# Seven block products of 256 columns in the last feed-forward stage of a decoder trunk

## The chip, the core and the metric

The program runs on one core of a Trainium2 chip. The metric is the device time of one execution in microseconds (us). A core has five engines that work from queues of their own: TensorE (PE, with PEld for its weight loads), VectorE (DVE), ScalarE (ACT), GpSimd (POOL) and SyncE (SP), which here only issues DMAs. PSUM is the memory that TensorE writes its products to; SBUF holds everything else.

## What is computed

The reference is a trunk of two layers on 512 tokens of width 1024. Each layer is a macaron: half a feed-forward, a mixer, half a feed-forward; a final RMSNorm ends it.

```python
def swiglu(h, w_in, w_out):
    gate, up = jnp.split(h @ w_in, 2, axis=-1)
    return (jax.nn.silu(gate) * up) @ w_out
...
x += 0.5 * swiglu(rmsnorm(x, g1), ffn1_w_in, ffn1_w_out)
x += mixer(rmsnorm(x, gm))          # layer 0: Mamba-2 scan, layer 1: S5
x += 0.5 * swiglu(rmsnorm(x, g2), ffn2_w_in, ffn2_w_out)
...
out = rmsnorm(x, final_norm)        # after layer 1
```

`w_in` is 1024 x 5632 (2816 gate columns, then 2816 up columns), `w_out` is 2816 x 1024. The change is in the last feed-forward, the second one of layer 1.

## The kernel before

The residual stream is kept transposed, in eight tiles `xT[0..7]` of 128 features x 512 tokens. The 2816 hidden features are 22 tiles of 128; the gate tile and the up tile of one number are here called a pair. Every fp32 operand of a large matmul is split in two fp32r halves, high and low, and a product is three matmuls: high x high, high x low, low x high (`proj`, L227 to L229). A weight block `wst` of eight 128 x 128 tiles comes by one DMA on SP's queue; ACT casts it to `whi` (L218) and DVE subtracts to get `wlo` (L220). There are four buffers for `wst` and three each for `whi` and `wlo`.

The function `ffn` goes through the 22 pairs in three parts (8, 7, 7). For each pair it runs 24 matmuls for the gate and 24 for the up rows into two PSUM tiles of the tag `mm` (four buffers), and DVE and ACT make `gt`, `up`, `ah`, `al` of them: `rbc`, the inverse RMS of each token, is multiplied in here (L262, L264), then Silu (L265), the gating product (L266), the cast `ah` (L268) and the remainder `al` (L270). After a part's pairs come its eight output rows: for each of the eight `xT` tiles the part's weight blocks are multiplied with the `ah` and `al` tiles, and DVE adds half of the result to `xT` (L277).

In the last stage every finished `xT` tile also goes to the final norm (`Prep.take`): its square on ACT (L171), its running sum on DVE (L176), its product with the final gain on ACT (`xg`, L1099), and then four transposes on PE and a copy on DVE that lay its rows out for the output (`rows`, L1104 and L1105). `nxt.flush()` runs the rows of the tile before at each step. After the last tile `sums` adds the squares up on PE (L148), `finish` runs a Newton iteration for the inverse root on DVE (L132 to L139), four scalings follow (L1257, L1259) and four output DMAs.

What sets the order: in this stage PE's order is the program's own order; ACT, DVE, POOL and SP are ordered by a planner.

Of the kernel before, what the change touches and what calls it, by code (L numbers as in the profile page):

```python
# [9 lines left out]
F32 = mybir.dt.float32  # L10
F32R = mybir.dt.float32r
I32 = mybir.dt.int32
AF = mybir.ActivationFunctionType
OP = mybir.AluOpType
AX = mybir.AxisListType

T = 512
D = 1024
KD = 8
# [11 lines left out]
def trunk_kernel(ctx, tc, x, ffn1_norm, ffn1_w_in, ffn1_w_out, mix_norm, ffn2_norm, ffn2_w_in, ffn2_w_out,  # L31
# [13 lines left out]
    def mm_ps():  # L45
        return psum.tile([128, 512], F32, tag="mm", name="mm", bufs=4)

    def aux_ps():
        return psum.tile([128, 512], F32, tag="aux", name="aux", bufs=4)
# [68 lines left out]
    def col(nm, j=0, n=1):  # L118
        i, r0 = C[nm]
        return cols[i][:, r0 + j:r0 + j + n]  # L120
# [39 lines left out]
    class Prep:  # L160


        def __init__(self, kind, gain, sink=None):
            self.kind, self.gain, self.sink = kind, gain, sink
            self.H, self.L = [None] * KD, [None] * KD
            self.acc = None
            self.later = []
# [25 lines left out]
        def sums(self):  # L193
            self.ps = compact_sum([self.acc, self.sq])

        def flush(self):
            while self.later:
                self.later.pop(0)()

        def finish(self):  # L200
            self.y4 = newton_rsqrt(self.ps[:, 0:4], 4, 1.0 / D)
            if self.kind == "hilo":
                self.rbc = work.tile([128, T], F32, name="rbc")
                S.copy(self.rbc, bcast_rows(self.y4))


    def fetch_w(src, kt, eng=None):
        st = wpool.tile([128, KD, 128], F32, name="wst", bufs=4)[:, :kt]
        i = (eng or nc.sync).dma_start(st, src.rearrange("(k p) c -> p k c", p=128))
        return st, i  # L210
# [5 lines left out]
    def split_w(st, kt):  # L216
        hi = wpool.tile([128, KD, 128], F32R, name="whi", bufs=3)[:, :kt]
        S.copy(hi, st)  # L218
        lo = wpool.tile([128, KD, 128], F32R, name="wlo", bufs=3)[:, :kt]
        V.tensor_tensor(lo, st, hi.bitcast(F32), op=OP.subtract)  # L220
        return hi, lo

    def proj(ps, w, H, L, first=True, last=True):
        hi, lo = w
        n = len(H)
        for k in range(n):
            PE.matmul(ps, hi[:, k], H[k], start=first and k == 0, stop=False)  # L227
            PE.matmul(ps, hi[:, k], L[k], start=False, stop=False)  # L228
            PE.matmul(ps, lo[:, k], H[k], start=False, stop=last and k == n - 1)  # L229


    def ffn(pr, w_in, w_out, nxt, fill=(), ready=(), done=(), early=None, pad=0):

        fill, ready, done = list(fill), list(ready), list(done)

        def pop():
            if fill:
                fill.pop(0)()

        with tc.tile_pool(name="ffn", bufs=2) as fp:  # L240
            if pad:
                fp.tile([128, pad // 4], F32, name="pad", bufs=1)
            for a, b in PARTS:
                AH, AL = [], []
                for f in range(a, b):
                    if done:
                        pg, pu = done.pop(0)
                    else:
                        pg, pu = mm_ps(), mm_ps()
                        wg = ready.pop(0) if ready else load_w(w_in[:, f * 128:(f + 1) * 128], KD)  # L250
                        proj(pg, wg, pr.H, pr.L)
                        if f == 0:
                            pr.sums()
                        wu = ready.pop(0) if ready else load_w(w_in[:, FF + f * 128:FF + (f + 1) * 128], KD)
                        proj(pu, wu, pr.H, pr.L)
                        if f == 0:
                            pr.finish()
                    if early and f == 0:
                        gt, up = early
                    else:  # L260
                        gt = fp.tile([128, T], F32, name="gt")
                        V.tensor_tensor(gt, pg, pr.rbc, op=OP.mult)  # L262
                        up = fp.tile([128, T], F32, name="up")
                        V.tensor_tensor(up, pu, pr.rbc, op=OP.mult)  # L264
                    S.activation(gt, gt, AF.Silu)  # L265
                    V.tensor_tensor(up, up, gt, op=OP.mult)  # L266
                    ah = fp.tile([128, T], F32R, name="ah", bufs=8)
                    S.copy(ah, up)  # L268
                    al = fp.tile([128, T], F32R, name="al", bufs=8)
                    V.tensor_tensor(al, up, ah.bitcast(F32), op=OP.subtract)  # L270
                    AH.append(ah)
                    AL.append(al)
                    pop()
                for d in range(KD):
                    po = mm_ps()
                    proj(po, load_w(w_out[a * 128:b * 128, d * 128:(d + 1) * 128], b - a), AH, AL)
                    V.scalar_tensor_tensor(xT[d], po, 0.5, xT[d], op0=OP.mult, op1=OP.add)  # L277
                    if b == FT:
                        nxt.flush()
                        nxt.take(d)  # L280
                    pop()
            while fill:
                fill.pop(0)()
        nxt.flush()
        if nxt.kind != "hilo":
            nxt.sums()
            nxt.finish()


    def ssd(pr, nxt):  # L290
# [804 lines left out]
    def fin_sink(d, g):  # L1095
        if "o" not in fin:
            fin["o"] = fin["p"].tile([128, 4, D], F32, name="fo", bufs=1)
        xg = fin["p"].tile([128, T], F32, name="xg")
        S.activation(xg, xT[d], AF.Copy, scale=g)  # L1099

        def rows():
            p = aux_ps()
            for t in range(4):
                PE.transpose(p[:, t * 128:(t + 1) * 128], xg[:, t * 128:(t + 1) * 128], ident)  # L1104
            V.tensor_copy(fin["o"][:, :, d * 128:(d + 1) * 128], p.rearrange("p (t c) -> p t c", t=4))  # L1105

        return rows
# [3 lines left out]

    def prep_for(st):
        if st is None:
            fin["p"] = ctx.enter_context(tc.tile_pool(name="fin", bufs=2))
            return Prep("final", ("fin", 0), fin_sink)
        if st == "ssd":
            return Prep("hilo", ("mix", 0))
        if st == "s5":
            s5["op"] = op_es.enter_context(tc.tile_pool(name="s5op", bufs=2))
            s5["up"] = up_es.enter_context(tc.tile_pool(name="s5u", bufs=2))  # L1120
            return Prep("s5", ("mix", 8), s5_sink)
        L = int(st[-1])
        return Prep("hilo", (st[:2], 8 * L))
# [22 lines left out]
    with tc.manual_schedule(engines={mybir.EngineType.Activation, mybir.EngineType.DVE, mybir.EngineType.PE}):  # L1146
# [14 lines left out]
        def part(i, j, k, n=1):  # L1161
            proj(done[i][j], [w_[:, k:k + n] for w_ in w[2 * i + j]], prep.H[k:k + n], prep.L[k:k + n], first=k == 0,
                 last=k + n == KD)
# [58 lines left out]
    for i, s in enumerate(stages[:-1]):  # L1222
        pr, prep = prep, prep_for(stages[i + 1])
        nxt = prep
        if s == "ssd":
            with tc.manual_schedule(engines=MAN):
                ssd(pr, nxt)
        elif s == "s5":
            with tc.manual_schedule(engines=MAN):
                s5_stage(pr, nxt)  # L1230
            op_es.close()
        else:
            L = int(s[-1])
            wi, wo = (ffn1_w_in, ffn1_w_out) if s[:2] == "f1" else (ffn2_w_in, ffn2_w_out)
            if s in s5_pre[:1]:
                ffn(pr, wi[L], wo[L], nxt, fill=pre0, ready=ready, done=done, early=early, pad=224)
                pre_es.close()
            elif s in s5_pre:
                with tc.tile_pool(name="pre1", bufs=2) as pp:
                    ffn(pr, wi[L], wo[L], nxt, fill=s5_setup(pp, 1))  # L1240
            elif stages[i + 1] == "s5":
                fill = [lambda: None] * 46
                for j in range(2):
                    for h in range(2):
                        fill[24 + 4 * h + 2 * j] = lambda j=j, h=h: out_ops(j, h)
                for j in range(2):
                    fill[40 + 2 * j] = lambda j=j: in_ops(j)
                fill[44] = lambda: out_ops(2, 0)
                for j in range(2 * NR):
                    fill[39 + 2 * j] = lambda j=j: res_w(j)  # L1250
                ffn(pr, wi[L], wo[L], nxt, fill=fill)
                up_es.close()
            else:
                ffn(pr, wi[L], wo[L], nxt)
    for t in range(4):
        if t % 2:
            V.tensor_scalar(fin["o"][:, t], fin["o"][:, t], prep.y4[:, t:t + 1], None, op0=OP.mult)  # L1257
# [32 lines left out]
```

## Time and profile before

| what | value |
|---|---|
| runs | 2084.42 us median of 3 (2082.14 to 2085.66) |
| profiled execution | 2085.69 us, span 2083.9 us, mean granted TensorE clock 0.989 |
| last feed-forward stage in the span | about 1709.8 us to the last matmul at 2069.3 us |
| end of the span behind the last matmul | 14.6 us: last `xT` tile, transposes, sum, Newton iteration, scaling, output DMA |
| matmuls of the stage | 22 pairs x 48 and 8 rows x 66, 128 x 512 each |

The page gives busy times by engine; a busy TensorE is an engine that has work in its pipeline, and the time that one matmul really takes is the distance between the starts of two that follow each other. The same holds for DVE and ACT, whose next instruction may begin shortly before the one ahead has ended.

### The profile page before, as it was taken

The page shows a single profiled execution, that of the slowest core. Times are in us where ns is not written, and L with a number is a line of the kernel's source. Part 1 is how long each engine was busy: PE and PEld are TensorE (multiplying, and loading weights), DVE is VectorE, ACT ScalarE, POOL GpSimd, SP SyncE. Part 2 cuts the span into 40 slices and gives each one's busy share as a digit, 9 for nine tenths or more (in the row PEclk, how much of TensorE's full clock was granted, in tenths as well). Part 3 has the DMA queues.
Part 4 walks back from the last instruction along what each step waited for, and adds up shares of the span by engine and source line. Part 5 has one row for each costly group of instructions (what it writes and reads, how often), then busy time and mean ns, then how long its engine had stood idle before and what let it go on. Part 6 is the DMA issues. An engine that isn't in the chain of part 4 may idle for free.

```text
span 2083.9 us, 26976 instructions
## 1 busy us (share of the span) xinstructions
PE 2034.2 (98%) x10675; PEld 1677.4 (80%) x10675; DVE 1252.0 (60%) x2119; ACT 789.2 (38%) x1140; POOL 84.0 (4%) x144
## 2 busy tenths in 40 slices
PE   8999999999999999999999999999997999999997
PEld 7888888878878877887788888888876888888886
DVE  6899345778775877568844544444468544444444
ACT  5323233466643664333423332222254333222223
POOL 1000000011110110000000000000011000000000
PEclk9999999999999999999999999999997999999999
DMA  6456633433343324445543353333367123333321
GB/s 167 117 140 172 168 100 85 124 106 99 114 117 97 94 74 149 125 121 163 143 137 87 105 192 100 93 94 99 98 196 235 56 87 102 99 96 87 110 84 59
DMA packets 411518, 244.28 MB, mean 117 GB/s; under 512 B 44952, under 2 KB 396864, under 8 KB 411136
## 3 DMA queue, kind: packets, MB, share of 16 engines
q1 hardware_dynamic: 381968, 203.19, 34.5%
q0 software_dynamic: 7984, 25.46, 3.8%
q10 hardware_dynamic: 21440, 13.91, 2.3%
q8 instruction: 84, 1.38, 0.3%
q14 instruction: 42, 0.34, 0.1%
HBM read 217.74 MB, written 24.25 MB: 116 GB/s over the span
## 4 chain that ended last, share of the span: by engine, by line
PE 59%; DVE 2%; ACT 1%; issue 1%; DMA 0%; DVEq 0%; ACTq 0%
PE mm L227 19%; PE mm L228 19%; PE mm L229 19%; DVE z L1007 0%; PE aux L228 0%; PE aux L227 0%; PE aux L229 0%; PE aux L865 0%; PE aux L871 0%; DMA tb<-d_t 0%; DVE z L1003 0%; DVE z L1005 0%; DVE z L1004 0%; PE aux L1025 0%; ACT z L1012 0%
## 5 line engine op out<-in xcount | busy, mean ns | idle before, releaser
L218 ACT CAST whi<-wst 128x1024 fp32r<-128x1024 f32 (+2 forms) x357 | 361.2, 1013 | 947.1 <-PE mm L228 669.9
L227 PE MATMUL mm<-hH,whi 128*128 128x512 f32 x1800 | 707.5, 393 | 0.0
L228 PE MATMUL mm<-hL,whi 128*128 128x512 f32 x1800 | 703.1, 391 | 0.0
L229 PE MATMUL mm<-hH,wlo 128*128 128x512 f32 x1800 | 701.8, 390 | 0.0
L220 DVE TENSOR_TENSOR wlo<-wst,whi 128x1024 fp32r<-128x1024 f32 (+2 forms) x357 | 418.8, 1174 | 68.8 <-ACT whi L218 65.0
L229 PEld LDWEIGHTS mm<-hH,wlo 128*128 128x128 f32 x1800 | 338.5, 188 | 71.5 <-issue 0.6
L227 PEld LDWEIGHTS mm<-hH,whi 128*128 128x128 f32 x1800 | 338.5, 188 | 71.3 <-issue 1.8
L228 PEld LDWEIGHTS mm<-hL,whi 128*128 128x128 f32 x1800 | 338.7, 188 | 69.3 <-issue 0.6
L228 PE MATMUL mm<-al,whi 128*128 128x512 f32 x704 | 274.6, 390 | 0.0
L229 PE MATMUL mm<-ah,wlo 128*128 128x512 f32 x704 | 274.2, 390 | 0.0
L227 PE MATMUL mm<-ah,whi 128*128 128x512 f32 x704 | 273.6, 390 | 0.0
L264 DVE TENSOR_TENSOR up<-mm,rbc 128x512 f32<-128x512 f32 x87 | 60.1, 691 | 214.9 <-PE mm L229 214.6
L277 DVE SCALAR_TENSOR_TENSOR xT<-mm,xT 128x512 f32<-128x512 f32 x96 | 66.1, 690 | 187.8 <-PE mm L229 187.7
L228 PEld LDWEIGHTS mm<-al,whi 128*128 128x128 f32 x704 | 132.2, 188 | 27.6 <-issue 0.6
L227 PEld LDWEIGHTS mm<-ah,whi 128*128 128x128 f32 x704 | 132.2, 188 | 27.6 <-issue 0.4
L229 PEld LDWEIGHTS mm<-ah,wlo 128*128 128x128 f32 x704 | 132.2, 188 | 27.4 <-issue 0.2
L262 DVE TENSOR_TENSOR gt<-mm,rbc 128x512 f32<-128x512 f32 x87 | 60.1, 690 | 151.5 <-PE mm L229 148.0
L387 DVE SCALAR_TENSOR_TENSOR cv<-raw,cols,cv 128x512 f32<-128x512 f32 x96 | 76.2, 804 | 7.0 <-ACT cv L385 6.4
L268 ACT CAST ah<-up 128x512 fp32r<-128x512 f32 x87 | 54.3, 624 | 58.2 <-DVE up L266 57.7
L266 DVE TENSOR_TENSOR up<-up,gt 128x512 f32<-128x512 f32 x87 | 60.1, 691 | 6.7
L270 DVE TENSOR_TENSOR al<-up,ah 128x512 fp32r<-128x512 f32 x87 | 59.5, 685 | 1.4 <-ACT ah L268 1.4
L265 ACT ACTIVATE gt<-gt 128x512 f32<-128x512 f32 x87 | 54.5, 627 | 8.5 <-DMA d_P<-p_ks 4.7
(330 smaller groups left out, 1714.7 us busy)
## 6 DMA issues: line engine op xcount, KB each, us to landing
wst<-in_ffn_w_in_dram SPq DMA_DIRECT2D x176, 512.0 KB, 3.9
wst<-in_ffn_w_out_dram SPq DMA_DIRECT2D x64, 448.0 KB, 3.7
wst<-in_ssd_in_proj_dram SPq DMA_DIRECT2D x48, 512.0 KB, 4.0
wst<-in_ffn_w_out_dram SPq DMA_DIRECT2D x32, 512.0 KB, 4.0
dec<-d_cs POOLq DMA_DIRECT2D x16, 512.0 KB, 4.4
opP<-d_P SPq DMA_DIRECT2D x16, 512.0 KB, 5.8
wst<-in_s_glu_w_dram POOLq DMA_DIRECT2D x12, 512.0 KB, 5.1
d_t<-p_cs POOLq DMA_DIRECT2D x8, 512.0 KB, 5.0
```

The lines of the kernel that those rows point to most:

```text
L218: S.copy(hi, st)
L220: V.tensor_tensor(lo, st, hi.bitcast(F32), op=OP.subtract)
L227: PE.matmul(ps, hi[:, k], H[k], start=first and k == 0, stop=False)
L228: PE.matmul(ps, hi[:, k], L[k], start=False, stop=False)
L229: PE.matmul(ps, lo[:, k], H[k], start=False, stop=last and k == n - 1)
L262: V.tensor_tensor(gt, pg, pr.rbc, op=OP.mult)
L264: V.tensor_tensor(up, pu, pr.rbc, op=OP.mult)
L265: S.activation(gt, gt, AF.Silu)
L266: V.tensor_tensor(up, up, gt, op=OP.mult)
L270: V.tensor_tensor(al, up, ah.bitcast(F32), op=OP.subtract)
L277: V.scalar_tensor_tensor(xT[d], po, 0.5, xT[d], op0=OP.mult, op1=OP.add)
L387: V.scalar_tensor_tensor(cv, raw[:, 1 + j:T + 1 + j], col("cw", j * 32 + ct), cv, op0=OP.mult, op1=OP.add)
```

## The change

A new function `ffn7` takes the place of `ffn` in the last stage alone. The parts are now 5, 4, 4, 4 and 5 pairs. The first part runs its five pairs as before. Meanwhile `build` makes from the finished `xT`, the gain and `rbc` seven blocks of 256 columns for each of four pairs of tiles (k and k + 4), and splits them in high (`th`) and low (`tl`) halves.

From pair 5 on, a pair is a 2 x 2 block product done in seven instead of eight block multiplications (Strassen's scheme in Winograd's form). The contraction is cut into tiles 0 to 3 and 4 to 7, the tokens into columns 0 to 255 and 256 to 511, and the gate and the up weights are the two block rows. With g0, g1 and u0, u1 for the halves of the two weight blocks, the seven weights are W1 = g0, W2 = g1, W4 = u1, W5 = u0 + u1, W6 = u0 + u1 + g0, W7 = u0 + g0 and W3 = u0 + u1 + g0 + g1. Each product (`mul`) is 12 matmuls of 128 x 256: four tiles, three matmuls each. The products are collected in three PSUM tiles `A`, `B` and `E`, and read off between them: `gt` after the first product of `A` (L482), `up` after its second (L505), `up` again after its third (L446).

The sums of weights come from two places. DVE adds u0 + u1 into a PSUM tile (`five`, L409) and adds g0 to it (`six`, L417). A DMA on POOL's queue with an addition in the transfer adds g0 onto u0 (`add7`) and g1 onto u0 + u1 + g0 (`add3`), both from SBUF to SBUF, 128 x 512 numbers each (L291). Each of W3 to W7 gets a cast on ACT (L401) and a remainder on DVE (L404); W1 and W2 are the halves of the ordinary split. The names of the steps (`s5`, `s3`, `s7`, ...) tell which weight they split. In `iteration`, `P` is the pair whose first products run, `N` the pair behind it, and `prev` the pair ahead, whose third and fourth products (W3, W4) and gating run inside the next pair's iteration.

All five engines now keep the program's own order in this stage. The final norm's rows run three tiles later (`nxt.flush(3)`), with four `xg` buffers instead of two; `rbc` has one buffer instead of two in the whole program; and the final norm's pool is opened when the seven blocks are no longer needed.

```diff
@@ Prep
-        def flush(self):
-            while self.later:
+        def flush(self, keep=0):
+            while len(self.later) > keep:
                 self.later.pop(0)()
...
-                self.rbc = work.tile([128, T], F32, name="rbc")
+                self.rbc = work.tile([128, T], F32, name="rbc", bufs=1)
...
+    def accumulate(dst, src):
+        G.dma_start(dst, src, accum_op=OP.add)
...
+        def mul(ps, w, j, first=False):
+            hi, lo = w
+            for k in range(4):
+                mh, ml = TH[k][:, j], TL[k][:, j]
+                PE.matmul(ps[:, c0], hi[:, k], mh, start=first and k == 0, stop=False, skip_group_check=True)
+                PE.matmul(ps[:, c0], hi[:, k], ml, start=False, stop=False, skip_group_check=True)
+                PE.matmul(ps[:, c0], lo[:, k], mh, start=False, stop=k == 3, skip_group_check=True)
...
+            def five(self):
+                self.x5 = aux_ps().rearrange("p (k c) -> p k c", k=4)
+                V.tensor_tensor(self.x5, self.u[:, 0:4], self.u[:, 4:8], op=OP.add)
+            def add7(self):
+                fetch_to(at["g", self.f])
+                self.g = raws[at["g", self.f]]
+                accumulate(self.u[:, 0:4], self.g[:, 0:4])
+            def six(self):
+                V.tensor_tensor(self.u[:, 4:8], self.x5, self.g[:, 0:4], op=OP.add)
+            def add3(self):
+                accumulate(self.u[:, 4:8], self.g[:, 4:8])
...
+        def iteration(i, prev, end, out):
+            P = pairs[i]
+            N = pairs[i + 1] if i + 1 < end else None
...
+            mul(P.A, P.W[1], 4, first=True)
+            if prev:
+                prev.acc_u4()
+                prev.c22()
+            split(j + 1)
+            if N:
+                N.s12()
+                N.s5()
+            S.copy(P.gt[:, c0], P.A[:, c0])
+            if prev:
+                mul(prev.A, prev.W[3], 6)
+                prev.silu0()
+                prev.silu1()
+            P.s3()
+            mul(P.B, P.W[2], 5, first=True)
+            if N:
+                N.s7()
+            V.tensor_tensor(P.gt[:, c0], P.gt[:, c0], P.B[:, c0], op=OP.add)
+            if i + 2 < end:
+                pairs[i + 2].five()
+                pairs[i + 2].add7()
+            if prev:
+                mul(prev.E, prev.W[4], 0)
+                prev.c21()
+                V.scalar_tensor_tensor(prev.up, prev.up, -1.0, prev.gt, op0=OP.mult, op1=OP.mult)
+            mul(P.A, P.W[6], 2)
+            if N:
+                N.s4()
+                N.six()
+            if prev:
+                halves_of(prev.up, out)
+            S.copy(P.up[:, c0], P.A[:, c0])
+            P.E = aux_ps()
+            mul(P.E, P.W[7], 3, first=True)
+            if N:
+                N.s6()
+                N.add3()
+            else:
+                split(j + 2)
+            mul(P.A, P.W[5], 1)
...
+                    steps = {0: ["five"], 1: ["s5"], 2: ["s4"], 3: ["add7", "six"], 4: ["s6", "add3"], 6: ["s7"],
+                             7: ["s12"]}
...
+                    if last:
+                        nxt.flush(3)
+                    elif d == KD - 1:
...
+                        pairs[b + 1].five()
+                        pairs[b + 1].add7()
...
-        xg = fin["p"].tile([128, T], F32, name="xg")
+        xg = fin["p"].tile([128, T], F32, name="xg", bufs=4)
...
-                ffn(pr, wi[L], wo[L], nxt)
+                with tc.manual_schedule(engines=MAN):
+                    ffn7(pr, wi[L], wo[L], nxt, ((0, 5), (5, 9), (9, 13), (13, 17), (17, 22)), late=late)
```

Up to the last stage the instructions stand in the same order on every engine in both programs. Three places in the last stage follow, as the built programs have them.

On PE, inside a pair of the last stage, before the change (`hH` and `hL` are the high and low halves of the input, `whi` and `wlo` those of the weights):

```order
L227 MATMUL mm<-hH,whi 128x512
L228 MATMUL mm<-hL,whi 128x512
L229 MATMUL mm<-hH,wlo 128x512
```

and with the change, at the step from `prev`'s fourth product to the sixth of the pair itself (`mh` and `ml` are the halves of W4, `hH` and `hL` those of W6, `th` and `tl` those of the input blocks):

```order
L371 MATMUL aux<-th,mh 128x256
L372 MATMUL aux<-tl,mh 128x256
L373 MATMUL aux<-th,ml 128x256
L371 MATMUL mm<-th,hH 128x256
L372 MATMUL mm<-tl,hH 128x256
L373 MATMUL mm<-th,hL 128x256
```

48 matmuls of 512 columns for a pair have become 84 of 256 columns, and two pairs' products alternate.

On DVE, one pair of the last stage before the change:

```order
L262 TENSOR_TENSOR gt<-mm,rbc 128x512
L220 TENSOR_TENSOR wlo<-wst,whi 128x1024
L264 TENSOR_TENSOR up<-mm,rbc 128x512
L266 TENSOR_TENSOR up<-up,gt 128x512
L220 TENSOR_TENSOR wlo<-wst,whi 128x1024
L270 TENSOR_TENSOR al<-up,ah 128x512
```

and with the change, one iteration with a pair ahead and a pair behind (the row with x2 is `s3` and `s7`; L409, `five`, stands behind L491 where a further pair of the part follows):

```order
L449 TENSOR_TENSOR up<-up,aux 128x256
L220 TENSOR_TENSOR wlo<-wst,whi 128x1024
L404 TENSOR_TENSOR hL<-aux,hH 128x512
L404 TENSOR_TENSOR hL<-wu,hH 128x512 x2
L491 TENSOR_TENSOR gt<-gt,mm 128x256
L458 TENSOR_TENSOR up<-up,aux 128x256
L498 SCALAR_TENSOR_TENSOR up<-up,gt 128x512
L404 TENSOR_TENSOR ml<-wu,mh 128x512
L417 TENSOR_TENSOR wu<-aux,wst 128x512
L384 TENSOR_TENSOR al<-up,ah 128x512
L404 TENSOR_TENSOR hL<-wu,hH 128x512
```

Before, two 1024-column remainders and four other instructions serve a pair; now one of them, five remainders of 512 and up to seven others, and the remainders of W3 and W7 stand ahead of the gating of the pair before.

On ACT, the same iteration with the change (L401 are the casts of the weight sums; the row with x2 is again `s3` and `s7`, whose sources come from the adding DMAs; L505 is the copy that must be done before PE adds the W5 product to `A`):

```order
L446 COPY up<-mm 128x256
L218 CAST whi<-wst 128x1024
L401 CAST hH<-aux 128x512
L482 COPY gt<-mm 128x256
L452 ACTIVATE gt<-gt 128x256
L455 ACTIVATE gt<-mm 128x256
L401 CAST hH<-wu 128x512 x2
L401 CAST mh<-wu 128x512
L382 CAST ah<-up 128x512
L505 COPY up<-mm 128x256
L401 CAST hH<-wu 128x512
```

Before, ACT had two casts of a weight block, the Silu and the cast `ah` for a pair. POOL had nothing to do in the last stage; now it issues 34 of the adding DMAs (L291), two for each of 17 pairs.

More of the change, by code (lines that the diff above doesn't have):

```diff
@@ L1113, in prep_for @@
         if st is None:
-            fin["p"] = ctx.enter_context(tc.tile_pool(name="fin", bufs=2))
             return Prep("final", ("fin", 0), fin_sink)
@@ L1253, in trunk_kernel, with late @@
             else:
-                ffn(pr, wi[L], wo[L], nxt)
+                def late():
+                    fin["p"] = ctx.enter_context(tc.tile_pool(name="fin", bufs=2, side="right"))
+                with tc.manual_schedule(engines=MAN):
+                    ffn7(pr, wi[L], wo[L], nxt, ((0, 5), (5, 9), (9, 13), (13, 17), (17, 22)), late=late)
     for t in range(4):
```

229 lines of the change are left out of this document (added).

## The prediction

> **What bounds the kernel now.** I read the page's busy shares and its chain of waits first, then the busy times of the last stage alone, then the timeline of one pair in it and of the end.
>
> ```profile
> PE 2034.2 (98%) x10675; PEld 1677.4 (80%) x10675; DVE 1252.0 (60%) x2119; ACT 789.2 (38%) x1140; POOL 84.0 (4%) x144
> PE 59%; DVE 2%; ACT 1%; issue 1%; DMA 0%; DVEq 0%; ACTq 0%
> core 0: us, PE busy (x) PEld busy (x) DVE busy (x) ACT busy (x) POOL busy (x), PEclk, DMA share, GB/s
> 1709.80:2069.30 359.50, 359.50 (x1657) 297.04 (x1658) 160.29 (x203) 103.20 (x127) 0.00 (x0) 1.00 0.30 87
> ```
>
> PE has work 98% of the span, and the chain is PE's. In the last stage (last row) PE is busy all 359.5 us at full clock, DVE 45%, ACT 29%, POOL not at all. So the stage is its matmuls, and fewer or shorter ones pay, as long as the engines with room keep up. What one pair takes:
>
> ```profile
> 1740.07 0.69 DVE L264 TENSOR_TENSOR up<-mm,rbc 128x512 f32<-128x512 f32 x1 [3.31 <-PE mm L229]
> 1750.95 0.69 DVE L264 TENSOR_TENSOR up<-mm,rbc 128x512 f32<-128x512 f32 x1 [3.31 <-PE mm L229]
> 1751.74 0.69 DVE L266 TENSOR_TENSOR up<-up,gt 128x512 f32<-128x512 f32 x1
> ```
>
> The same step of two pairs (first two rows) is 10.88 us apart: 48 matmuls, 0.2267 each. 22 pairs and 528 matmuls of the output rows make 239.4 + 119.7 = 359.1 of the 359.5 us.
>
> **The change: the products.** 17 pairs go from 48 x 0.2267 = 10.88 us to 84 matmuls of 256 columns, which the trace lacks. Nearest rows:
>
> ```profile
> 422.57 1.05 PE L434 MATMUL aux<-CT,BT 128*128 128x128 f32 x8
> 422.35 1.08 PEld L434 LDWEIGHTS aux<-CT,BT 128*128 128x128 f32 x8
> 430.14 1.46 PE L464 MATMUL aux<-wx,btok 128*128 128x256 f32 x6
> L434 PE MATMUL aux<-CT,BT 128*128 128x128 f32 x64 | 8.4, 274 | 0.0
> L464 PE MATMUL aux<-wx,btok 128*128 128x256 f32 x48 | 11.6, 378 | 0.0
> ```
>
> Less the last one's own length, these plain fp32 matmuls start (1.05 - 0.274) / 7 = 0.111 us apart for 128 columns and (1.46 - 0.378) / 5 = 0.216 for 256. An fp32r matmul passes 512 columns in 0.2267, so 256 of its columns stream about as long as those 128, each with a full weight load: 0.111 is the lower end, and the 0.19 us loads overlap. The upper end keeps the whole surplus of 0.2267 over 0.216 for each matmul: 0.122. I take half of 0.2267, 0.1133, near the lower end and of the same kind. A product of 12 is then 1.36 us, a pair 9.52, and 17 pairs gain 23.2 us (10.8 at 0.122, 26.5 at 0.111).
>
> [...]
>
> **DVE's and ACT's work in an iteration.** Durations, and how close two can follow:
>
> ```profile
> 1586.08 0.69 DVE L1003 TENSOR_TENSOR z<-aux,tb 128x512 f32<-128x512 f32 x1 [0.51 <-ACT z L1002]
> 1586.69 0.68 DVE L1004 TENSOR_TENSOR z<-z,tb 128x512 f32<-128x512 f32 x1
> L220 DVE TENSOR_TENSOR wlo<-wst,whi 128x1024 fp32r<-128x1024 f32 x49 | 59.9, 1223 | 9.4 <-ACT whi L218 9.3
> L474 DVE TENSOR_TENSOR st<-st,aux 128x256 f32<-128x256 f32 x16 | 6.7, 416 | 0.1
> L268 ACT CAST ah<-up 128x512 fp32r<-128x512 f32 x22 | 13.7, 625 | 13.5 <-DVE up L266 13.5
> ```
>
> DVE starts the next instruction 0.09 us before the last ends: 0.60 for 512 columns, 1.13 for 1024, 0.33 for 256. Where it needs the last one's result it starts 0.79 behind (1750.95 and 1751.74 above). On ACT I take off the same: 0.53, 0.96, 0.28. An iteration has nine DVE instructions of 512, three of 256 and one of 1024: 5.4 + 1.0 + 1.1 = 7.5 us, under PE's 9.5. ACT has some 5.6. By its amount of work neither can bound; by its order it can.
>
> **The adding DMAs** are what the order hangs on. `s3` casts what `add3` made; on ACT `s7`, `s4`, `ah` and the `up` copy are queued behind that cast, on DVE the remainders of W3 and W7, the sum into `gt`, `five` and the gating; and PE's W5 product waits for the `up` copy. `add3` itself waits for `s6`'s remainder, the last DVE step of the iteration before. No DMA of the trace adds. Plain ones:
>
> ```profile
> d_ER<-p_rER POOLq DMA_DIRECT2D x1, 256.0 KB, 2.7
> d_EI<-p_rEI POOLq DMA_DIRECT2D x1, 256.0 KB, 2.3
> wst<-in_s_glu_w_dram POOLq DMA_DIRECT2D x12, 512.0 KB, 5.1
> wst<-in_ssd_out_proj_dram SPq DMA_DIRECT2D x16, 256.0 KB, 2.7
> wst<-in_ssd_in_proj_dram SPq DMA_DIRECT2D x48, 512.0 KB, 4.0
> ```
>
> POOL's 256 KB land in 2.3 to 2.7 us; 256 KB more cost SP's loads 1.3. [...]
>
> [...]
>
> **The steady iteration.** From the end of `s6`'s remainder: the add, the cast (0.53 + 0.14), then on DVE W3, W7, `gt`, `five`, `c21`, gating, W4, `six`, `al`, W6: eight of 0.60, two of 0.33, and 0.4 for results that a next step or POOL waits for. The loop is add + 6.5 us: 9.6 at 3.1, against PE's 9.52. So it costs 0.1 now, and each us beyond 3.0 comes in whole.
>
> **Start of a part.** Here DVE arrives late, since the last output rows give it `five` of the next pair, whose `add7` only then goes out. With 0 at PE's first product of pair 13: `five` ends at 1.4, the add lands at 4.6, `s7` is cast to 5.2, `s4` to 5.7, and the `up` copy ends at 6.0, where PE has been ready for W5 since 5.44: it waits 0.66. DVE ends `s6` at 9.4 where PE began the second pair at 7.46; the copy that frees `A` costs 0.26; add at 12.6, W3 to gating until 16.5, `ah`, `up` copy at 17.4: W5 waits 1.65. Three parts of four pairs lose 2.57 each: 7.7 us. The part at pair 5 is worse. Building the seven blocks costs DVE for each of the four pairs of tiles six steps of 256 columns, one of 512 and remainders of 1024 and 768: 2.0 + 0.6 + 2.0 = 4.6, 18 us in all, and 6.6 of it stands in the output rows. There, behind the third row, DVE has 4.8 (additions) + 3.7 (five splits) + 6.6 + 5.3 (weight steps) = 20.4 us, PE five rows of 3.4 = 17.0. So the `gt` copy, behind a cast that waits for `five`, ends 2.16 after PE is ready for W6; then 0.94, 0.26 and 1.65 as above: 5.0 us. In the part of five one more 0.13.
>
> **Output rows.** Parts of 4 and 5 pairs keep the matmuls, and each part's fourth row waits for its split, since the first three rows hold all three `whi` buffers until their last matmuls: cast and remainder take 0.5 + 0.14 + 0.6 (0.7 with five tiles), and the second and third row's last matmuls cover 1.36 less the hops. That leaves 0.2 in parts of four and 0.44 in parts of five, 1.5 us in all. DVE's 16 more additions (16 x 0.60) lie under PE's 21.8 us of rows a part; uncovered they would be 9.6 us.
>
> **Nothing, with the cover.** The first five pairs: building runs on DVE beside 54 us of matmuls, of which it used 45%. One `rbc` buffer: its five copies come after a stage's first products, when the old one has no reader left. SP carries the same bytes; its `u` loads wait for the `s3` two iterations back, and the gate loads behind them have an iteration of 9.5 us against 4.0. The end:
>
> ```profile
> 2069.33 0.69 DVE L277 SCALAR_TENSOR_TENSOR xT<-mm,xT 128x512 f32<-128x512 f32 x1 [2.49 <-PE mm L229]
> 2069.94 0.68 DVE L1105 COPY fo<-aux 128x512 f32<-128x512 f32 x1
> 2070.65 0.71 ACT L1099 ACTIVATE xg<-xT,cols 128x512 f32<-128x512 f32 x1
> 2071.41 0.66 PE L1104 MATMUL aux<-ident,xg 128*128 128x128 f32 x4 [1.68 <-ACT xg L1099]
> 2072.10 0.69 DVE L1105 COPY fo<-aux 128x512 f32<-128x512 f32 x1 [1.48 <-PE aux L1104]
> ```
>
> Between 2069.94 and 2072.10 DVE has one copy; three late rows put three there, 1.8 us into 2.1: hidden; uncovered, two more copies, 1.2 us.
>
> **Sum:** -23.2 + 7.7 + 5.0 + 0.13 + 1.5 = -8.9 us. The profiled execution took 2085.69 (span 2083.9), so it would be 2076.8; the runs' median is 1.3 lower, so 2075.5.
>
> **Rivals.** (1) *The add lands late.* Nothing in the trace shows an adding transfer, and each iteration waits for one. At 3.9 us the gain is gone; beyond, 17 loops pay a us each: at 5.1 the sum is +19.0, 2103.4. For it: POOL's 512 KB row. Against: POOL's 256 KB rows, and DMA engines 30% busy. (2) *The add lands as fast as POOL's plain 256 KB*, 2.5: the waits of the parts' starts shrink by 0.6 each, the sum is -13.8, 2070.6. (3) *Each matmul keeps a fixed surplus* (0.122): 10.8 us of gain, PE's iteration is 10.2 and hides the adds, waits 9.6: -1.2, 2083.2, no change. For it: 0.2267 against 0.216 at equal streaming.
>
> **How the numbers follow.** Chances: forecast 0.40, late add 0.24, fast add 0.23, fixed surplus 0.13. Time 2075.5. The forecast's own range is 2070 to 2081 (adds of 2.6 to 3.6). For 8 in 10: down to 2063, where the fast add meets 0.111 per matmul (-17.5, 2066.9) and some of the parts' first waits fall away with it; up to 2100, an add of 4.9. A measurement of this kernel tells about 0.2% from no change: below 2080.3 is faster, above 2088.6 slower. Faster: 0.36 + 0.22 + 0.02 = 0.60. Slower: 0.22. Same: 0.18.
>
> **What would show it.** In the profile after: starts of the 128x256 matmuls 0.113 apart within a product; the issue row of `wu<-wst` on POOL with 3.1 us; the cast L401 waiting for that DMA; PE waiting for ACT's `up` copy L505, most in each part's second pair; iterations of 9.6 us; the end unchanged. I am wrong if PE's waits sit in other places, on DVE's amount of work or on splits, or if the adds take over 4 us.

## The result, and the profile after

The changed kernel takes 2097.8 us (median of 4 runs, 2095.93 to 2098.52) against 2084.06 us (2082.14 to 2085.66): ratio 1.0065, 95% interval 1.0048 to 1.0082. It is slower by 13.7 us, where 8.9 us less were forecast. The profiled execution has a span of 2096.1 us, 12.2 more than before.

The page, in the order in which the prediction read the one of before: busy shares, the chain of waits, the costliest wait of the new matmuls, and two rows of DMA issues (last number: median us to landing).

```profile
PE 2028.2 (97%) x11287; PEld 1699.1 (81%) x11287; DVE 1333.5 (64%) x2306; ACT 843.6 (40%) x1300; POOL 112.8 (5%) x178
PE 50%; DVE 5%; issue 3%; DMA 3%; ACT 2%; POOL 0%; POOLq 0%; ACTq 0%; DVEq 0%
L371 PE MATMUL mm<-th,hH 128*128 128x256 f32 x204 | 60.2, 295 | 15.7 <-ACT up L505 15.1 <-ACT gt L482 0.6
...
wu<-in_ffn_w_in_dram SPq DMA_DIRECT2D x17, 512.0 KB, 6.0
wu<-wst POOLq DMA_DIRECT2D x34, 256.0 KB, 3.8
```

PE is still busy 97% of the span, but the chain holds 50% of PE instead of 59%: it now runs through DVE, ACT and DMAs. The third row, the first matmuls of the W6, W5 and W3 products, names the wait: nearly all of it is W5 products that stand behind ACT's `up` copy. The 15.7 us of this group count from the modelled end of the matmul ahead; from start to start, and over all groups, PE's waits in the products are 17.4 us (below).

How close the new matmuls start, in the timeline of PE at the start of pair 5:

```profile
1788.79 0.28 PE L371 MATMUL mm<-th,whi 128*128 128x256 f32 x1
1788.90 0.28 PE L372 MATMUL mm<-tl,whi 128*128 128x256 f32 x1
1789.02 0.28 PE L373 MATMUL mm<-th,wlo 128*128 128x256 f32 x1
1789.14 0.28 PE L371 MATMUL mm<-th,whi 128*128 128x256 f32 x1
```

They start 0.120 us apart (the median over the stage), not 0.113. What PE waits for, first as the chain of waits passes the start of the part at pair 5 (start, duration, what), then in ACT's timeline, then PE's next matmul:

```profile
1791.72 5.81 DMA wu<-wst
...
1802.84 3.25 DMA wu<-wst
```

```profile
1797.56 0.62 ACT L401 CAST hH<-wu 128x512 fp32r<-128x512 f32 x1 [4.72 <-DMA wu<-wst]
1798.08 0.61 ACT L401 CAST mh<-wu 128x512 fp32r<-128x512 f32 x1
1798.60 0.36 ACT L505 COPY up<-mm 128x256 f32<-128x256 f32 x1
```

```profile
1799.02 0.58 PE L371 MATMUL mm<-th,hH 128*128 128x256 f32 x1 [3.51 <-ACT up L505]
```

The reader is to see the queue: ACT's `up` copy is short and its input has long been ready, but two casts stand ahead of it, and the first waits for `add7` of the next pair, which takes 5.8 us to land. `add3` of that pair, the same number of bytes on the same queue 11 us later, takes 3.25. SP's queue tells what was different (timeline of SP: start, duration of the issues, count):

```profile
1789.99 4.42 SPq L396 DMA_DIRECT2D wu<-in_ffn_w_in_dram  x3
```

Three loads of 512 KB go out at 1789.99, 1792.02 and 1793.78, around the issue of `add7` at 1791.72. Behind the longest waits stands something that no view of before had in this stage (stretches of time: PE's busy time and count, ..., the granted clock third from last):

```profile
1795.40:1798.80 3.40, 0.10 (x1) 0.00 (x0) 0.59 (x1) 1.24 (x3) 0.00 (x0) 1.00 1.13 286
1798.80:1802.20 3.40, 3.18 (x15) 3.19 (x16) 2.68 (x6) 1.00 (x3) 0.84 (x1) 0.51 0.50 115
...
1932.00:1935.40 3.40, 1.03 (x8) 1.03 (x9) 1.84 (x4) 1.41 (x3) 0.00 (x0) 1.00 1.13 299
1935.40:1938.80 3.40, 3.40 (x18) 3.40 (x17) 2.49 (x5) 2.26 (x4) 1.47 (x2) 0.50 0.55 103
```

A stretch of 3.4 us in which TensorE hardly works is followed by one in which it gets half its clock. It happens three times (1798.8, 1867.1, 1935.4); the 47 matmuls that start in there are 0.214 us apart on average and cost 4.4 us.

The end of the program, in DVE's timeline:

```profile
2076.25 0.69 DVE L176 TENSOR_TENSOR acc<-acc,sq 128x512 f32<-128x512 f32 x1 [0.76 <-ACT sq L171]
2076.86 0.68 DVE L1453 COPY fo<-aux 128x512 f32<-128x512 f32 x1
2077.46 0.68 DVE L578 SCALAR_TENSOR_TENSOR xT<-mm,xT 128x512 f32<-128x512 f32 x1
2078.90 0.69 DVE L176 TENSOR_TENSOR acc<-acc,sq 128x512 f32<-128x512 f32 x1 [0.76 <-ACT sq L171]
2079.51 0.69 DVE L1453 COPY fo<-aux 128x512 f32<-128x512 f32 x1
2080.11 0.68 DVE L578 SCALAR_TENSOR_TENSOR xT<-mm,xT 128x512 f32<-128x512 f32 x1
```

PE's last 512-column matmul starts at 2078.26. Before, the last addition to `xT` began 0.44 us behind it (2068.89, 2069.33); now 1.85, because DVE does the sum and the copy of the tile ahead first, and the sum waits for ACT's square. From that matmul to the end it is 17.8 us instead of 15.0.

Together, from start to start against the spans (us):

| term | forecast | profile after |
|---|---|---|
| products, 17 x (84 x 0.120 - 10.88) | -23.2 | -13.6 |
| PE's waits in the parts at pairs 5 / 9 / 13 / 17 | 5.0 + 2.6 + 2.6 + 2.7 = 12.8 | 4.8 + 4.7 + 4.3 + 3.6 = 17.4 |
| matmuls right behind a wait, some 0.1 each | 0 | 1.4 |
| half clock behind three of them | 0 | 4.4 |
| output rows' split waits | 1.5 | 0.9 |
| first product of the stage | 0 | 0.6 |
| the end | 0 | 2.8 |
| ahead of the stage | 0 | -0.8 |
| two groups of transposes now behind the last 512-column matmul, and the rest | 0 | -0.9 |
| sum | -8.9 | 12.2 (spans: 12.2) |

The last row of terms is what the spans leave over. The stage's first product waits 0.6 us for the last `hL` of its input (L186, to 1709.88); before, PE ran matmuls of the sum of squares (L148) in that wait.

### The profile page after: what moved, and what is told of

Its sections match the earlier page's. It is cut to its first block, busy times and chain, and to the rows that moved or that the text cites. A ratio compares the mean times of both kernels' runs of the same rounds, so it can differ in the third digit from the quotient of the medians.

```text
span 2096.1 us, 28686 instructions
## 1 busy us (share of the span) xinstructions
PE 2028.2 (97%) x11287; PEld 1699.1 (81%) x11287; DVE 1333.5 (64%) x2306; ACT 843.6 (40%) x1300; POOL 112.8 (5%) x178
## 4 chain that ended last, share of the span: by engine, by line
PE 50%; DVE 5%; issue 3%; DMA 3%; ACT 2%; POOL 0%; POOLq 0%; ACTq 0%; DVEq 0%
PE mm L227 15%; PE mm L228 15%; PE mm L229 14%; DMA wu<-wst 2%; PE mm L371 1%; PE mm L373 1%; PE mm L372 1%; DMA wst<-in_ffn_w_in_dram 1%; DVE wlo L220 1%; DVE hL L404 1%; DVE z L1355 0%; DVE xT L578 0%; ACT hH L401 0%; POOL wu L291 0%; PE aux L373 0%
## 5 line engine op out<-in xcount | busy, mean ns | idle before, releaser
L218 ACT CAST whi<-wst 128x1024 fp32r<-128x1024 f32 (+3 forms) x356 | 346.1, 973 | 737.0 <-PE mm L228 518.4
L227 PE MATMUL mm<-hH,whi 128*128 128x512 f32 x1528 | 601.9, 394 | 0.1
L228 PE MATMUL mm<-hL,whi 128*128 128x512 f32 x1528 | 597.4, 391 | 0.3 <-DVE hL L186 0.3
L229 PE MATMUL mm<-hH,wlo 128*128 128x512 f32 x1528 | 596.3, 390 | 0.0
L220 DVE TENSOR_TENSOR wlo<-wst,whi 128x1024 fp32r<-128x1024 f32 (+3 forms) x356 | 400.3, 1125 | 90.3 <-ACT whi L218 86.4
L229 PEld LDWEIGHTS mm<-hH,wlo 128*128 128x128 f32 x1528 | 287.5, 188 | 60.7 <-issue 0.6
L228 PEld LDWEIGHTS mm<-hL,whi 128*128 128x128 f32 x1528 | 287.7, 188 | 59.5 <-DVE hL L186 0.6
L371 PE MATMUL mm<-th,hH 128*128 128x256 f32 x204 | 60.2, 295 | 15.7 <-ACT up L505 15.1
L404 DVE TENSOR_TENSOR hL<-wu,hH 128x512 fp32r<-128x512 f32 x51 | 34.4, 689 | 46.2 <-ACT hH L401 45.3
L373 PE MATMUL mm<-th,hL 128*128 128x256 f32 x204 | 59.0, 289 | 0.0
L372 PE MATMUL mm<-tl,hH 128*128 128x256 f32 x204 | 58.9, 289 | 0.0
```

The source lines that it names most:

```text
L371: PE.matmul(ps[:, c0], hi[:, k], mh, start=first and k == 0, stop=False, skip_group_check=True)
L372: PE.matmul(ps[:, c0], hi[:, k], ml, start=False, stop=False, skip_group_check=True)
L373: PE.matmul(ps[:, c0], lo[:, k], mh, start=False, stop=k == 3, skip_group_check=True)
L404: V.tensor_tensor(lo, src, hi.bitcast(F32), op=OP.subtract)
```

## The experiments

Theory A: the waits come from a queue place on ACT and an add that lands late. B: DVE is simply behind at a part's start by its amount of work. C and its rival are on the half clock, D and E on the end, F and G on why the adds are late, H on the matmul. Differences are against the kernel before, run on the same chip at the same time; the changed kernel has +13.7.

**1. The cast that waits goes last.**

```diff
             mul(P.B, P.W[2], 5, first=True)
-            if N:
-                N.s7()
...
                 N.s6()
                 N.add3()
+                N.s7()
```

> One step moved, same work: the cast and remainder of W7 (s7) of the next pair go behind add3 at the end of an iteration, so that on ACT the up copy no longer stands behind a cast that waits for an add. Theory A (queue place and a late add): the long waits before the W5 products at the parts' starts (3.79, 3.89, 2.84, 1.64 us and 0.55 to 1.72 in the second pairs, 17.4 us with the rest of the products' waits) fall to about 3 us in all, and the three stretches at half clock (4.35 us) go with them: about 2079.5. Rival B (DVE is simply behind at a part's start, by its amount of work): the order on ACT changes nothing, 2095 to 2099.

Measured: 2085.49 us, +0.7; ratio 1.0007 (0.9998 to 1.0016). Moving one cast takes 13 us off the changed kernel: A, not B. But the waits fell to some 8 us, not 3. Group of the waiting matmuls, and the chain of waits at the part of pair 13:

```profile
L371 PE MATMUL mm<-th,hH 128*128 128x256 f32 x204 | 59.2, 290 | 7.7 <-ACT up L503 5.7 <-ACT up L446 1.4 <-ACT gt L482 0.6
```

```profile
1924.27 6.46 DMA wu<-wst
```

The next late transfer takes over: `add3` of the second pair, 6.46 us, and `s3`'s cast behind it. Two stretches at half clock stay (3.0 us).

**2. The adds on DVE.**

```diff
     def accumulate(dst, src):
-        G.dma_start(dst, src, accum_op=OP.add)
+        V.tensor_tensor(dst, dst, src, op=OP.add)
```

> add3 and add7 become additions on DVE (two more instructions of 0.6 us in each iteration, no adding transfer). Theory A: with an add of 0.7 us instead of 3.3 to 6.2 us the waits at the parts' starts fall to 3 or 4 us in all, DVE's 7.5 + 1.2 = 8.7 us stay below PE's 10.1 us of an iteration: about 2079 to 2080. Rival B: DVE is what is late at a part's start, so 1.2 us more for each iteration make it later: 2098 to 2105.

Measured: 2083.10 us, -1.6; ratio 0.9994 (0.9985 to 1.0002), not told apart from the kernel before. No stretch at half clock is left in the stage. DVE's amount of work was never the limit: 34 more instructions there (23.5 us busy in all) made the changed kernel 15 us faster. Each part keeps waits of 0.4 to 1.1 us, from start to start, at the same copies (7.0 us in all, 5.4 by the modelled ends in the group below), and the split in the rows before pair 5, where DVE has the building to do, costs PE 1.2 us instead of 0.6.

```profile
L371 PE MATMUL mm<-th,hH 128*128 128x256 f32 x204 | 58.8, 288 | 5.4 <-ACT up L505 2.8 <-ACT up L446 1.7 <-ACT gt L482 0.9
```

**3. Work in the wait.**

```diff
             P.E = aux_ps()
+            if not prev and i < 17:
+                mul(P.E, P.W[6], 2, first=True)
+                mul(P.E, P.W[6], 2, first=True)
             mul(P.E, P.W[7], 3, first=True)
```

> 24 extra products of 256 columns (2.9 us at 0.120) into the tile E ahead of the first pair's W7 product in the parts that start at pairs 5, 9 and 13, where PE waits 3.79, 3.89 and 2.84 us behind that product; W7's first matmul then starts the tile anew. Theory C (TensorE gets half its clock after a wait of some 3 us): the waits that remain are 0.9, 1.0 and 0, the stretches at half clock go, 4.35 us less: 2093.5. Rival: the half clock has another cause (the denser matmuls, say) and stays: 2097.8, or later if the extra products do not fit.

Measured: 2095.36 us, +10.6; ratio 1.0052 (1.0040 to 1.0065). The three stretches at half clock are gone (below, where before they were 0.51 and 0.50), although 72 matmuls of the same dense kind were added: C. Of the time, less came back than expected: the first pairs' waits shrank, those of the second pairs grew, since these hang on adds and not on PE.

```profile
1798.80:1802.20 3.40, 3.40 (x27) 3.21 (x28) 2.68 (x6) 1.40 (x3) 0.84 (x1) 1.00 0.27 48
...
1935.40:1938.80 3.40, 3.40 (x31) 3.40 (x30) 2.23 (x4) 2.02 (x5) 0.84 (x1) 1.00 0.60 102
```

**4. Rows one tile late.**

```diff
-                        nxt.flush(3)
+                        nxt.flush(1)
```

> The final norm's rows run one tile later instead of three. Theory D (the end is 2.2 us longer because the last xT tile waits on DVE behind the running sum of the tile before, which waits for ACT; the three copies lie inside ACT's and PE's time behind it): no change, within 0.5 us of 2097.8. Rival E (the two more copies at the end are uncovered): 1.2 to 2.2 us less, 2095.6 to 2096.6.

Measured: 2102.43 us, +17.7; ratio 1.0086 (1.0072 to 1.0100). Neither theory had that. PE's timeline shows it:

```profile
2058.04 0.39 PE L229 MATMUL mm<-ah,wlo 128*128 128x512 f32 x1
2060.45 0.66 PE L1452 MATMUL aux<-ident,xg 128*128 128x128 f32 x4 [2.02 <-ACT xg L1447]
2063.79 1.11 PE L1452 MATMUL aux<-ident,xg 128*128 128x128 f32 x4 [2.69 <-ACT xg L1447]
2064.56 0.78 PE L227 MATMUL mm<-ah,whi 128*128 128x512 f32 x1
```

The first three rows of a part end together. Rows one tile late put the transposes of the first two tiles right behind, and PE waits for additions, squares and products that have only begun; then it runs at half clock (0.43 us a 512-column matmul) for a while. From the last 256-column matmul to the last one of 512 columns it is 34.8 us here and 26.8 in the changed kernel, so "three tiles later" avoids 8 us there. The end, from the last matmul, is 15.5 us here instead of 17.8, but DVE had time to catch up in PE's waits, so D and E stay open.

**5. The running sum one tile late, with rows one tile late.** The additions wait in a list, `due`, and are taken from it behind the next tile's addition to `xT`:

```diff
-                V.tensor_tensor(self.acc, self.acc, sq, op=OP.add)
+                self.due.append(lambda: V.tensor_tensor(self.acc, self.acc, sq, op=OP.add))
```

> Rows one tile late as in the run before, and the running sum of a tile's squares on DVE behind the next tile's addition, so that DVE does not wait for ACT between them. Theory D (DVE's order, with ACT's square in the chain, makes every row 3.4 us on DVE, as long as PE's row, so that DVE never catches up): DVE is on time for each row, PE's transposes do not wait, the end from the last matmul of 512 columns falls from 17.8 to some 15.5 us: 2095.5. Rival: DVE's amount of work in the rows is too much, and the 4.6 us of the rows run one late stay: 2102.

Measured: 2103.03 us (one execution). As the run before: PE's waits behind the third row are the same 2.4 and 3.0 us from start to start, so the sum's place does not matter there. It tells nothing on the end.

**6. The same with rows three tiles late, as in the changed kernel.**

> The changed kernel, rows three tiles late as there, with the running sum of a tile's squares on DVE behind the next tile's addition. Theory D (the end is late because DVE's row is a chain through ACT's square as long as PE's row): the last addition to xT starts within 0.6 us of its matmul's end instead of 1.6, the end from the last matmul of 512 columns falls from 17.8 to some 16.5 us. Rival E (the late rows' copies are what the end pays for): it stays at 17.8.

Measured: 2096.28 us (one execution), and the end is 15.7 us from the last 512-column matmul instead of 17.8. DVE's timeline:

```profile
2079.16 0.69 DVE L581 SCALAR_TENSOR_TENSOR xT<-mm,xT 128x512 f32<-128x512 f32 x1 [0.54 <-PE mm L232]
2079.77 0.68 DVE L177 TENSOR_TENSOR acc<-acc,sq 128x512 f32<-128x512 f32 x1
2080.37 2.47 DVE L1458 COPY fo<-aux 128x512 f32<-128x512 f32 x4
2082.76 0.15 DVE L132 TENSOR_SCALAR nw_v<-aux 128x4 f32<-128x4 f32 x1
```

The last addition starts 0.43 us behind its matmul (2078.73) again: D. The late rows' copies now follow without a gap up to the Newton iteration; the 0.7 us that the end is still longer than before may be theirs, which this run does not show.

**7. The loads of the up weights later.** From pair 8 on they are issued by ACT at the end of an iteration:

```diff
-                nc.sync.dma_start(self.u, w_in[:, j:j + 128].rearrange("(k p) c -> p k c", p=128))
+                (nc.scalar if f > sevens[0] + 2 else nc.sync).dma_start(self.u, w_in[:, j:j + 128].rearrange("(k p) c -> p k c", p=128))
...
-            new_pair()
             fetch_to(j + 3)
...
             mul(P.A, P.W[5], 1)
+            new_pair()
```

> From pair 8 on the loads of the up weights are issued on ACT's queue at the end of an iteration, in the program's order, instead of on SP's queue as soon as a buffer is free; everything else as changed. Theory F (the adds at a part's start are late because 512 KB loads run beside them): the add7 of the second pairs lands in 3.3 to 4.2 us instead of 5.8, 6.2, 4.9 and 4.0; PE's wait behind it was 2.1 to 2.4 us shorter than the landing each time, so the four waits shrink from 12.2 to 6 us and the half clock (4.35) goes: about 2087. Rival G (an adding transfer from SBUF to SBUF is slow by itself at that place): landings and time stay, 2096 to 2099.

Measured: 2100.35 us, +15.4; ratio 1.0070 (1.0058 to 1.0082). The transfers did as F says in three of four parts: `add7` of the second pairs landed in 4.7, 4.0 and 3.4 us instead of 6.2, 4.9 and 4.0. The fourth (pair 6) still had a load of SP beside it and took 6.9. But the time did not follow: the loads now ran beside the `add3` of the second pairs. These were issued 1.5, 0.9 and 0.6 us earlier in their parts, but took 5.5, 3.9 and 3.9 us to land instead of 3.8, 3.3 and 3.3, so that they landed no earlier; and PE, held less ahead of them, waited there 3.9, 2.3 and 2.3 us instead of 1.0, 0.5 and 1.7. Moving the collision moved the wait:

```profile
L371 PE MATMUL mm<-th,hH 128*128 128x256 f32 x204 | 60.9, 298 | 18.3 <-ACT up L504 17.7 <-ACT gt L481 0.6
```

**8. Copies that do not add.**

```diff
-        G.dma_start(dst, src, accum_op=OP.add)
+        G.dma_start(dst, src)
```

> The two transfers of add7 and add3 copy and no longer add (the additions are left out, so W3 and W7 are not the sums they should be); same bytes, same queue, same order. Theory F: the adding costs little, undisturbed landings go from 3.3 to some 2.5 us and the disturbed ones at the parts' starts stay at 4 to 5.5 us; time 2090 to 2095. Rival G (the adding is what is slow): the landings at the parts' starts fall to 2.3 to 2.7 us like the plain 256 KB of the kernel before, the waits to 1 to 2 us, no half clock: 2084 to 2086.

Measured: 2089.41 us, +4.5; ratio 1.0019 (1.0010 to 1.0029), between the two expectations. The transfers from issue to landing, adding (the changed kernel), then plain (this one):

```profile
DMA to landing us min/median/max: 3.2/3.8/7.8
```

```profile
DMA to landing us min/median/max: 2.3/2.6/5.3
```

By the shortest landings, adding costs 0.9 us more than copying the same 256 KB; beside loads both are late (the copy up to 5.3, the adding one up to 7.8). So F and G each hold a part, and 9 of the 13.7 us hang on the adding. How the two share at a given place stays open, since the loads also stand elsewhere when the adds are faster.

**9. 256 columns without block products.** In the kernel before, for the gate and the up rows of pairs 5 to 21, 24 matmuls for each half of the columns:

```diff
-                        proj(pg, wg, pr.H, pr.L)
+                        proj_cols(pg, wg, pr.H, pr.L, 2)
```

> The kernel before, with the gate and up products of pairs 5 to 21 of the last stage in two pieces of 256 columns (96 matmuls for 48 a pair), nothing else. Theory H (a matmul of 256 columns starts 0.120 us behind the last, 13 ns above half of 0.2267, whatever is around it): 17 x (96 x 0.120 - 48 x 0.2267) = 10.8 us more, 2095. Rival (0.1133 a matmul, as the prediction took, and the 0.120 comes from the block products' own operands): no change, 2084.

Measured: 2097.00 us, +12.1; ratio 1.0055 (1.0041 to 1.0068). PE's timeline:

```profile
1780.01 0.28 PE L237 MATMUL mm<-hH,whi 128*128 128x256 f32 x1
1780.13 0.28 PE L238 MATMUL mm<-hL,whi 128*128 128x256 f32 x1
1780.25 0.28 PE L239 MATMUL mm<-hH,wlo 128*128 128x256 f32 x1
```

0.120 us apart, without a wait in 1632 matmuls: H. The distance goes with the shape, not with the block products' operands.

**10. 128 columns**, the same with 4 pieces.

> The kernel before, with the gate and up products of pairs 5 to 21 of the last stage in four pieces of 128 columns (192 matmuls a pair). Theory H1 (each matmul costs its columns plus a fixed 13 ns): starts 0.0667 us apart, 17 x (192 x 0.0667 - 10.88) = 32.6 us more, 2117. Rival H2 (the weight load, 0.19 us and overlapped by two, sets a floor near 0.11): 0.11 apart, 17 x (21.1 - 10.88) = 174 us more, 2259.

Measured: 2265.03 us (one execution). PE's timeline:

```profile
1790.04 0.28 PE L238 MATMUL mm<-hL,whi 128*128 128x128 f32 x1
1790.15 0.28 PE L239 MATMUL mm<-hH,wlo 128*128 128x128 f32 x1
1790.26 0.28 PE L237 MATMUL mm<-hH,whi 128*128 128x128 f32 x1
```

0.1115 us apart (median): H2's price. That the weight load is what sets it was not tested by itself. An estimate from the two distances measured at 512 and 256 columns is (0.2267 - 0.120) / 256 = 0.417 ns a column and 13 ns for each matmul; by that, 128 columns would be 0.067 apart, and the 0.1115 measured show that something else sets the pace there.

**11. All causes at once.** Adds of pairs 6 to 21 on DVE, `s7` and `s5` behind the copies that PE waits for, `ah` behind the `up` copy, the sum one tile late, rows three tiles late until the last two tiles, which take two each:

```diff
+            V.tensor_tensor(dst, dst, src, op=OP.add)
...
             S.copy(P.gt[:, c0], P.A[:, c0])
+            if N:
+                N.s5()
...
+            S.copy(P.up[:, c0], P.A[:, c0])
             if prev:
                 halves_of(prev.up, out)
-            S.copy(P.up[:, c0], P.A[:, c0])
...
-                        nxt.flush(3)
+                        nxt.flush(3 if d < 6 else 8 - d)
```

> The changed kernel with the causes found so far taken away: the adds of pairs 6 to 21 on DVE, W7's and W5's casts of the next pair (s7, s5) behind the copies that PE waits for, the cast ah behind the up copy, the running sum of squares behind the next tile's addition, and the last rows spread over the last two tiles. Theory A with H: of PE's waits in the products some 2 us are left, no half clock, rows' split waits 1 us, the end 1 to 2 us shorter than in the changed kernel: -13.6 + 2 + 1.7 + 1 = 9 us less than before, 2076. Rival B (DVE, with two more instructions in each iteration, is what bounds the parts' starts): no better than the run with the adds on DVE alone, 2083.

Measured: 2076.92 us, -7.6; ratio 0.9954 (0.9941 to 0.9968): A, not B. PE still waits 2.0 us at the second pair of the part at pair 5 and 0.4 in each later part, and one stretch at half clock costs 1.4. The five executions fall into two groups, three from 2076.9 to 2077.6 and two at 2072.4 and 2072.8; only one of the first was profiled, so what the other two lack is not shown.

**12. Two more steps moved.** `five` and `add7` of the pair after the next to the iteration's end, `s7` into the pair's own iteration (against run 11):

```diff
             if prev:
+                P.s7()
                 mul(prev.A, prev.W[3], 6)
...
-            if i + 2 < end:
-                pairs[i + 2].five()
-                pairs[i + 2].add7()
...
                 N.add3()
-                N.s7()
             else:
                 split(j + 2)
+            if i + 2 < end:
+                pairs[i + 2].five()
+                pairs[i + 2].add7()
```

> The reordered kernel once more with two steps moved: u0 + u1 and the add of W7 of the pair after the next (five, add7) to the end of an iteration, behind the steps that the next pair's first products wait for, and W7's split (s7) into the pair's own iteration, behind the copies. In the run before, PE still waited 2.16 us (1.49 us more by half clock behind it) for the second pair of the part at pair 5, where DVE stood at five, which waited for its load, and 0.42 us in each later part behind s7's cast. Theory A: these 2.0 + 1.5 + 1.2 us go: 2072. Rival: the waits move to the next late step, five's reader or W7's product: 2075 to 2077.

Measured: 2072.09 us, -13.7; ratio 0.9938 (0.9924 to 0.9951). Its chain of waits and the group that waited 15.7 us in the changed kernel:

```profile
PE 59%; DVE 2%; issue 1%; ACT 1%; DMA 0%; SPq 0%; DVEq 0%; ACTq 0%
```

```profile
L377 PE MATMUL mm<-th,hH 128*128 128x256 f32 x204 | 57.7, 283 | 0.0
```

No product waits, no stretch at half clock is left in the stage, and the chain is PE's again, 59% as before the change. That the -13.7 us of the medians equal the products' -13.6 is in part luck: the profiled execution, the slowest of the five, has a span 12.1 us shorter than before. In it the rows' split and the stage's first product still cost 1.2 us, and PE begins the stage 1.3 us later than in the profile before.

## Why the prediction was wrong, point by point

- **The products (-23.2): the largest error, 9.6 us.** The step that failed is "I take half of 0.2267, 0.1133, near the lower end". The upper end, with the whole surplus kept, was 0.122, and 0.120 was measured, in the kernel before too (9). The lower end rested on 128-column fp32 matmuls at 0.111, read as streaming; run 10 shows nearly that value, 0.1115, for 128-column pieces in fp32r as well, so the 0.111 may not have been streaming and could not bound 256 columns. The third rival named the size; its own sum failed with the other terms.
- **DVE's and ACT's work in an iteration: right.** 8.7 us with the adds on DVE still lie under PE's 84 x 0.120 = 10.1 (2, 12).
- **The adding DMA (3.1 us): right undisturbed (3.2), wrong where it counts.** Even the 3.1 was near in part by luck: 2.5 for a plain copy and 0.6 for the adding were taken. No run shows the 0.6 (half of the 1.3 us that 256 KB more cost SP's loads); the shortest landings of run 8 give 2.3 for the copy and 0.9 for the adding in its place. The median was 3.8, and the second pairs' `add7` took 5.8, 6.2, 4.9 and 4.0 us. I had one duration for all places, while 512 KB loads of the next pairs go out as soon as buffers are free (at 1789.99, 1792.02 and 1793.78 around the `add7` of 5.8 us). The steady loop itself holds: with PE's longer iteration the adds there are nearly hidden, as that rival said: 1.7 of the 17.4 us of waits fall behind a part's second pair.
- **Start of a part (12.8): mechanism right, size and place not.** PE waits for the `up` copy behind a cast behind an add, as forecast. But in three of the four parts the worst wait was the first pair's W5, not the second's: 3.7 us against 0.94 at pair 5, and 3.8, 2.7 and 1.5 against 0.66 in the others. 17.4 us were measured, 4.6 more.
- **Half clock: missing from the sum, 4.4 us.** It hangs on those waits (1, 2, 3).
- **Output rows (1.5): 0.9.** Near.
- **The end ("nothing, with the cover"): 2.8 us.** The late copies were hidden in the changed kernel, under DVE's lateness; the step that failed is to have looked at the copies alone. In a fixed order the running sum with its wait for ACT comes ahead of the next tile's addition. DVE's addition of the fourth row starts 5.8 us behind PE's last matmul of that row (2067.98, 2062.23); its next rows take 3.4 us and the last two 2.65, against PE's 3.9, so it has not caught up at the end. Run 6 took 2.1 of the 2.8 away.
- **The first rival (late add)** named the right mechanism, with a price (every loop pays) that is not what happened: nearly only the parts' starts pay.

## What to carry to other kernels

In a hand-written order, put nothing that waits for a DMA ahead of the short copy for which TensorE waits; a cast in the wrong place cost 13 us here, its move nothing. Cost a transfer at the place where it runs, with the loads that a free buffer sets off beside it (an add of 256 KB landed in 3.2 us undisturbed and in 5.8 beside three loads), and ask of each wait of more than 2 us what it does to TensorE's clock (half clock behind three of them cost 4.4 us here). Cutting columns in half did not halve a matmul: the starts were 0.2267 us apart at 512 columns, 0.120 at 256 and 0.1115 at 128.

## What the hardware showed that I had not expected

In the records of the changed kernel TensorE's clock is granted in stretches of 3.41 us: the three at half clock begin at 1798.83, 1867.10 and 1935.37, 20 times 3.41 us apart, and last 3.41 us each. In the profiles of all runs, from 1000 us of the span on, a stretch at full clock in which PE was idle for 1.2 to 1.82 us, by the modelled ends of its matmuls, was never followed by half clock (0 of 38); one with 2.0 us or more always was (79 of 79); from 1.88 to 1.99 us, 8 of 9 were. In the profiles before and after alone it is 0 of 6 from 1.04 to 1.60 us and 13 of 13 from 1.97 to 3.32. Ahead of 1000 us the bound lies lower at one place: in the profile before, the stretch from 760.26 on has 1.81 us of idle PE, and half clock follows it. So a wait of little more than 2 us is enough if it falls into one stretch, here in the run with plain copies (1.42 us of PE's work, then 0.51 of the clock):

```profile
1873.00:1876.40 3.40, 1.42 (x13) 1.22 (x12) 3.33 (x7) 1.03 (x3) 0.54 (x1) 1.00 0.69 202
1876.40:1879.80 3.40, 3.40 (x16) 3.40 (x17) 1.68 (x4) 1.07 (x3) 0.54 (x1) 0.51 0.43 140
```

A wait of 2.7 us that lay across two stretches cost nothing more (run 4, at 1930.7).
